# A two-layer hybrid mixer trunk: the first norm in two halves among the modulation loads, modulation by quarters, four c gates ahead of the scans' output, and later side steps

## The chip, the core and the metric

The kernel runs on one core of a Trainium2 chip. A core has five engines with queues of their own: TensorE (PE, matmuls; PEld is its weight load), VectorE (DVE), ScalarE (ACT), GpSimd (POOL) and SyncE (SP, which here only issues DMAs). The metric is the time of one execution on the device in microseconds, the median of several runs. The profile is of one such execution. TensorE's clock has two levels, 1.2 and 2.4 GHz; the profile gives the granted clock of a stretch as a share of the higher.

## The reference, cut to what matters

128 context tokens and 512 latent tokens of width 1024 go through two layers with the same weights; they are one block of 640 columns in the kernel. A layer is:

```python
sh1, sc1, g1, sh2, sc2, g2 = split(silu(c) @ w_mod + b_mod, 6)   # one row for context, one for latent
h = rmsnorm(x, norm1_g) * (1 + sc1) + sh1
proj = h @ w_in                                  # q k v, z, beta, a, hyena, fnet, gates a b c
y_a = delta_mixer(...)    # gated DeltaNet, chunks of 64, forward and backward scan
y_b = hyena_mixer(...)    # two long convolutions by FFT, filters from a small sine MLP
y_c = fourier_mixer(...)  # FNet
x = x + g1 * ((sig(ga) * (y_a @ w_pa) + sig(gb) * (y_b @ w_pb) + sig(gc) * (y_c @ w_pc)) @ w_o)
h = rmsnorm(x, norm2_g) * (1 + sc2) + sh2
x = x + g2 * (silu(h @ w_gate) * (h @ w_up)) @ w_down
```

The latent tokens first get a position embedding (`xs = x_sample + grid_pos_embed`). At the end stands one more rmsnorm; the final DeltaNet states of the context are an output too.

## The kernel before

Everything is transposed: the 1024 channels lie on 8 blocks of 128 partitions, the 640 tokens in the free dimension, in two chunks c=0 and c=1 of 320. A *main tile* is one weight tile of 128 output channels against all tokens. Operands are split in a high and a low part, and three products are added, so that a tile takes 8 x 3 x 2 = 48 matmuls of 128x320 into the PSUM tiles `pg`. Weights arrive in `wr` by SyncE's queue; `wh` (ScalarE) and `wl` (GpSimd, or an adding DMA that GpSimd issues) are their two parts. `_stream` lists the main tiles in the order in which they are run: `ba` and the q, k, v tiles (stage `qkv`), the FNet inputs and z (`fn`), twelve hyena tiles (`hy`), eight a gates (`ga`), two c gates, the merges of a, the rest of the c gates with the merges of c, b gates, merges of b, the o tiles, and the feed-forward half.

All other work is written as Python generators, *side steps*, in which each `yield` ends a step. `bg` puts one into a list; `pump`, called at several points of every main tile, takes those steps whose time `co.t` (plus the `hint` that was yielded) has come by the planner's own clock, up to a budget, and writes their instructions behind what is there. `on(...)` sets `co.t` to the time at which the planner expects the named tiles, and `self.cur.t += n` puts a step n of its microseconds later. All this happens while the program is written: on the chip each engine runs its own queue strictly in order, and semaphores tie the queues together. `finish` writes the remaining steps of a generator with no main tile between them.

The side steps of interest:
- `mods` computes the modulation `mod` (columns of w_mod against silu(c)): per group of four blocks two halves of small matmuls `ps<-A,ct`, a copy of the row by ScalarE into `U`, and two small matmuls (`ps<-small,U`, in `turn`) that turn it back into `mod`. With `first=True` 16 blocks are loaded ahead at the start; else 1 MB is loaded into one buffer for each half of a group.
- `embed` adds the positions to x and sums the squares (`sq_add`); `rstd` sums them over channels on TensorE (`ps<-small,T` 128x1), takes the rsqrt on VectorE with twelve tiny instructions (`nm`, `nr`, `rs`) and spreads it over the partitions with TensorE (`rb`, one tile `ps` per chunk); `norm` makes the gain `na` from `mod` and the normed tiles in high and low part.
- `filters` makes the hyena filters: a sine MLP (`sin_mlp`), then many steps of 2 to 6 matmuls.
- `delta_gates`, `delta_qk` (its `one(t)` normalises and transposes q and k for one of five blocks of tokens), `delta_unit` (the decay and key products of a chunk: GpSimd passes over 512 columns into `U`, matmuls with `stcr`, an exponential, products), `prep` (with `delta_inv`: inverses, on VectorE) and `scan` (33 numbered steps, each a few matmuls and VectorE operations, each needing the one before).
- `merge` multiplies a projected branch by its gate and adds it up; the last branch's sum is halved and split for the o tiles (`split`).

In `run`, the steps of `embed`, `mods` and `filters` before the first main tile are taken by `finish_one` in the planner's order, and the norm of x is begun only after that.

## Time and profile before

| | |
|---|---|
| median of three runs | 2749.7 us (2746.98 to 2753.47) |
| the profiled execution | 2748.93 us, its span 2747.2 us, granted clock 0.963 in the mean |
| TensorE busy | 2542.1 us, 93% of the span |
| VectorE / ScalarE / GpSimd busy | 1784.8 / 1101.5 / 1272.3 us, 65 / 40 / 46% |
| DMA | 353.57 MB, 129 GB/s in the mean |

TensorE is what the time is made of; the other engines matter where it waits for them. The idle time in front of a matmul, and what ended it, stands in brackets in TensorE's timeline. A busy time of TensorE has the clock in it: at the lower level the same matmul takes about twice as long.

The stages by time: start 0 to 54.4; layer 0: `qkv` to 239.9, `fn` to 325.0, `hy` to 467.1, `ga` to 557.1, then `dfin` (end of the scans, c gates), merges and gates, o tiles from 869.7 to 933.8, feed-forward half to 1398.5; layer 1: `qkv` to 1571.5, `fn` to 1669.5, `hy` to 1797.7, `ga` to 1916.5, o tiles from 2222.0 to 2285.8, feed-forward half to 2735.1.

### The profile page before, as it was taken

How to read it: one execution, taken by the hardware profiler on the slowest of the kernel's cores; microseconds unless marked ns; L12 is line 12 of the kernel's file. 1: busy time of each engine (PE TensorE's matmuls, PEld its weight loads, DVE VectorE, ACT ScalarE, POOL GpSimd, SP SyncE). 2: the span in 40 equal slices, each digit the busy share in tenths (PEclk: the TensorE clock that was granted, in tenths of full speed). 3: DMA queues.
4: the chain of work that ended last, by engine and by line, in shares of the span. 5: the costliest groups of instructions: out<-in, count | busy, mean ns of one | idle time of the engine just before them, and what ended most of it. 6: DMA issues, size and time to landing. Idle time of an engine off the chain costs nothing. (4 is left out here: it accounts for less than half of the span.)

```text
span 2747.2 us, 55957 instructions
## 1 busy us (share of the span) xinstructions
PE 2542.1 (93%) x22520; PEld 2411.4 (88%) x22520; DVE 1784.8 (65%) x3375; ACT 1101.5 (40%) x2383; POOL 1272.3 (46%) x1228
## 2 busy tenths in 40 slices
PE   5897999979999999999988989889999999999998
PEld 3786988979999999999977779778889998999997
DVE  5467977444645686667665789665456358777775
ACT  4454464422332343333335544534223333444442
POOL 2334325332335576666632352333333365776662
PEclk8998999989999999999989999989999999999999
DMA  7442663534554235422222437425255441222222
GB/s 295 171 164 63 162 146 90 155 134 146 204 191 169 62 128 173 162 78 85 85 97 90 144 79 184 115 65 159 95 200 193 163 167 47 85 85 77 85 76 79
DMA packets 125683, 353.57 MB, mean 129 GB/s; under 512 B 11994, under 2 KB 26330, under 8 KB 118944
## 3 DMA queue, kind: packets, MB, share of 16 engines
q1 hardware_dynamic: 107856, 312.76, 34.2%
q0 software_dynamic: 17568, 37.24, 7.1%
q8 instruction: 177, 2.90, 0.4%
q14 instruction: 82, 0.67, 0.1%
HBM read 288.60 MB, written 37.24 MB: 119 GB/s over the span
## 5 line engine op out<-in xcount | busy, mean ns | idle before, releaser
L2189 PE MATMUL pg<-A,wh 128*128 128x320 f32 (+1 forms) x6304 | 1456.0, 318 | 44.3 <-POOL A L2189 10.4
L2189 PEld LDWEIGHTS pg<-A,wh 128*128 128x128 f32 (+1 forms) x6304 | 1070.5, 192 | 87.0 <-POOL A L2189 18.0
L2189 PE MATMUL pg<-A,wl 128*128 128x320 f32 (+1 forms) x3152 | 990.5, 314 | 2.3 <-DMA wl<-wr 1.8
L2189 POOL TENSOR_TENSOR wl<-wr,wh 128x512 fp32r<-128x512 f32 (+2 forms) x374 | 524.3, 1415 | 513.8 <-ACT wh L2189 486.4
L2189 PEld LDWEIGHTS pg<-A,wl 128*128 128x128 f32 (+1 forms) x3152 | 603.5, 191 | 7.1 <-DMA wl<-wr 4.2
L2189 ACT CAST wh<-wr 128x512 fp32r<-128x512 f32 (+2 forms) x486 | 287.0, 609 | 278.8 <-PE pg L2189 231.4
L2189 PE MATMUL ps<-A,wh 128*128 128x320 f32 x1696 | 378.8, 310 | 0.0
L2189 PEld LDWEIGHTS ps<-A,wh 128*128 128x128 f32 x1696 | 283.9, 188 | 1.4 <-issue 1.0
L2189 PE MATMUL ps<-A,wl 128*128 128x320 f32 x848 | 263.5, 311 | 5.0 <-POOL wl L2189 4.8
L2189 POOL TENSOR_TENSOR wl<-U,wh 128x512 fp32r<-128x512 f32 x160 | 227.8, 1441 | 43.5 <-ACT wh L2189 43.5
L2189 POOL DMA_DIRECT2D wl<-wr x112 | 98.7, 912 | 277.7 <-ACT wl L2189 264.6
L2189 PE MATMUL ps<-A,A 32*32 32x32 f32 (+5 forms) x2984 | 205.3, 239 | 9.3 <-DVE A L2189 5.5
L2189 PEld LDWEIGHTS ps<-A,A 32*32 32x32 f32 (+2 forms) x2984 | 177.3, 142 | 20.2 <-DVE A L2189 6.0
L2189 DVE TENSOR_TENSOR T<-T,T 128x320 f32<-128x320 f32 (+1 forms) x139 | 133.6, 961 | 83.7 <-ACT T L2189 79.4
L2189 POOL TENSOR_TENSOR A<-A,A 128x640 fp32r<-128x640 f32 (+5 forms) x84 | 122.2, 1473 | 121.0 <-ACT A L2189 113.1
L2189 DVE TENSOR_TENSOR A<-A 128x120 f32<-128x120 f32 (+23 forms) x690 | 161.0, 297 | 14.0 <-DMA A<-hyS 10.8
L2189 PEld LDWEIGHTS ps<-A,wl 128*128 128x128 f32 x848 | 159.7, 188 | 7.4 <-POOL wl L2189 7.3
L2189 ACT CAST wh<-U 128x512 fp32r<-128x512 f32 x160 | 99.2, 621 | 165.4 <-PE ps L2189 60.0
L2189 PE MATMUL pg<-A,A 128*128 128x320 f32 x1056 | 161.0, 310 | 0.0
L2189 PEld LDWEIGHTS pg<-A,A 128*128 128x128 f32 x1056 | 156.3, 188 | 0.7 <-issue 0.2
L2189 DVE STREAM_TRANSPOSE A<-A 32x1024 f32<-32x1024 f32 x72 | 151.2, 2120 | 1.5
L2189 DVE TENSOR_TENSOR U<-ps,U 128x512 f32<-128x512 f32 x144 | 77.9, 542 | 103.3 <-PE ps L2189 66.8
(165 smaller groups left out, 3194.7 us busy)
## 6 DMA issues: line engine op xcount, KB each, us to landing
wr<-in_wbig_dram SPq DMA_DIRECT2D x272, 512.0 KB, 3.7
A<-in_wmod_dram SPq DMA_DIRECT2D x40, 1024.0 KB, 6.4
A<-hT SPq DMA_DIRECT2D x32, 1024.0 KB, 7.7
wl<-wr POOLq DMA_DIRECT2D x112, 256.0 KB, 4.5
kSp<-U SPq DMA_DIRECT2D x40, 256.0 KB, 2.0
U<-kSp SPq DMA_DIRECT2D x40, 256.0 KB, 8.7
A<-in_wmod_dram SPq DMA_DIRECT2D x16, 512.0 KB, 10.2
hyS<-T SPq DMA_DIRECT2D x24, 320.5 KB, 3.1
```

Of the source, the lines that this page charges most:

```text
L2189: return f(*a, **k)
```

## The change

- *Start.* `embed` is one step now, with all sums of squares; silu(c) is issued behind the table loads only; the groups of `mods` go in the order 0, 8, 4, 12, each turned at once. `norm` runs in two halves (`halves=True`): gain and tiles for channels 0 to 3 of both chunks between the groups, for 4 to 7 behind them. The order of the first steps is written out by hand in `run`. x is stored to DRAM (`xS`) behind the first tile's first chunk.
- *Modulation by quarters.* Outside the start a group is four steps with a load of 512 KB each, into two halves of a buffer in turn; the load of the next quarter is issued before the step of this one.
- *Four c gates* stand in front of the output of the scans; the first two c merges follow one another.
- *Merges by chunks.* The last branch's split is done for each chunk of 320; the factor 0.5 goes into the modulation gate `g`.
- *GpSimd.* The passes of `delta_unit` are three steps now instead of one; one subtraction of `filters` goes from VectorE to GpSimd.
- *Later steps.* `cur.t += 1.5` to `3.0` in `rstd` (not the first), `filters` of layer 1 (whose MLP is also cut into more steps), `delta_qk`, `delta_gates`, `delta_unit`, `hyena`.

The core of the diff:

```diff
 def _stream():
-    s += [gate("c", 0), gate("c", 1)]
+    s += [gate("c", m) for m in range(4)]
     s += [("pa", m) for m in range(0, 8, 2)]
-    s.append(("pc", 0))
-    for m in range(2, 8, 2):
+    s += [("pc", 0), ("pc", 2)]
+    for m in range(4, 8, 2):
         s += [gate("c", m), gate("c", m + 1), ("pc", m)]
...
 def mods(self, l, lo, hi, par=False, hint=0.5, first=False):
+        nq = 2 if first else 4
+        w1 = D // nq
...
+            js = js[::2] + js[1::2]
...
+            todo = [(j, h) for j in range(lo, hi, 4) for h in range(nq)]
+
+            def load():
+                j, h = todo.pop(0)
+                w = S[:, h % 2 * D:h % 2 * D + D]
+                nc.sync.dma_start(w.rearrange("p (g c) -> p g c", g=4),
+                                  self.I["wmod"][l, j:j + 4, :, h * w1:h * w1 + w1].rearrange("g p c -> p g c"))
...
-                    w = [S[:, g * 512:g * 512 + 512] for g in range(4)]
-                    nc.sync.dma_start(S[:, :2048].rearrange("p (g c) -> p g c", g=4),
-                                      self.I["wmod"][l, j:j + 4, :, h * 512:h * 512 + 512].rearrange("g p c -> p g c"))
+                    w = [S[:, h % 2 * D + g * w1:h % 2 * D + g * w1 + w1] for g in range(4)]
+                    if todo:
+                        load()
...
 def rstd(self, u, n, w):
         self.on(self.ssq[:, u:u + n * w])
+        if u:
+            self.cur.t += 3.0
         yield 0.0
...
 def norm(self, l, gcol, sh, scl, new, place, halves=False):
-        for c in range(2):
+        for k0, c in ((k0, c) for k0 in range(0, KD, n) for c in range(2)):
             yield from self.wait(c)
-            new(c)
-            for k in range(2):
+            if k0 == 0:
+                new(c)
+            if halves and c == 0:
+                gain(k0, n)
+            for k in range(k0, k0 + 2):
                 head(k, c)
...
 def filters(self, l):
+            if l:
+                self.cur.t += 3.0
             yield
+        for sl in (slice(0, TS), slice(TS, T)):
...
 def delta_unit(self, N, Pm, u, s, t):
             rhs.append(r)
+            self.cur.t += 1.5
+            yield
         E, mb = N[:, u], Pm[u]
...
+        yield
         ps = self.ps()
...
 def merge(self, br, m, th, first, last):
+                if last:
+                    hi, lo = [x[(m + i) // 4][:, (m + i) % 4][:, sl] for x in self.mgs]
+                    self.split(hi, lo, mt[:, sl], nc.vector if m == 6 else None)
                 self.pump()
-            if last:
-                hi, lo = self.mgs[0][(m + i) // 4][:, (m + i) % 4], self.mgs[1][(m + i) // 4][:, (m + i) % 4]
-                nc.vector.tensor_scalar(out=mt, in0=mt, scalar1=0.5, scalar2=None, op0=ALU.mult)
-                self.split(hi, lo, mt)
...
 def run(self):
+        self.rs, self.hn = [n, n], 0
+        co = self.co = self.bg(self.norm_mod(0, C_G1, 0, 8, True))
+        ff = self.ff
+        for x in (m, cd, ff, n, ff, m, m, n, n, ff, m, m, n, *[co] * 4, m, m):
+            self.step(x)
+        self.free(0, 0)
+        for x in (*[co] * 4, ff):
+            self.step(x)
+        while not m.done:
+            self.step(m)
```

How rows stand in the queues, at three places. First, VectorE at the start. `mod` is the modulation, `nm` and `nr` belong to the rsqrt, `T<-small,nr` is the tile that TensorE then spreads over the partitions, `na` is the gain, `U<-A,ps` the first normed tile. Before:

```order
L2189 TENSOR_TENSOR mod_114<-ps_371,par_90 128x2x4
L2189 TENSOR_TENSOR T_157<-T_157,T_374 128x640
L2189 TENSOR_TENSOR mod_114<-ps_395,par_90 128x2x4
L2189 TENSOR_SCALAR nm_404<-ps_398 128x5
L2189 TENSOR_SCALAR nr_405<-nm_404 128x5
L2189 TENSOR_TENSOR rs_407<-nr_405 128x5
...
L2189 TENSOR_TENSOR T_418<-small,nr_405 128x640
L2189 SCALAR_TENSOR_TENSOR na_446<-mod_114,par_90 128x8 x2
L2189 TENSOR_TENSOR U_453<-A_103,ps_420 128x320
L2189 TENSOR_TENSOR U_455<-A_103,ps_420 128x320
```
After, where the rows left out are the rsqrt's and two of the filters' sine:

```order
L2246 TENSOR_TENSOR mod_113<-ps_233,par_90 128x2x4
L2246 CAST stcr<-small 128x256
L2246 TENSOR_SCALAR nm_244<-ps_238 128x5
L2246 TENSOR_SCALAR nr_245<-nm_244 128x5
L2246 TENSOR_TENSOR rs_247<-nr_245 128x5
...
L2246 TENSOR_TENSOR T_258<-small,nr_245 128x640
L2246 TENSOR_SCALAR U_264<-U_263 128x512
...
L2246 TENSOR_SCALAR U_263<-U_263 128x512
L2246 TENSOR_TENSOR mod_113<-ps_312,par_90 128x2x4
L2246 SCALAR_TENSOR_TENSOR na_319<-mod_113,par_90 128x4 x2
L2246 TENSOR_TENSOR U_326<-A_106,ps_315 128x320
```
The rsqrt now stands behind the first `mod` group instead of the fourth, the gain is made of four columns behind the second group instead of eight behind the fourth, and the first tile follows it.

Second, GpSimd in `fn1`. The passes of a unit are `U<-dgh,small` (two) and `<-small,dsel`, `MEMSET A` clears the storage they end in, `DMA wl<-wr` adds a weight tile's low part. Before:

```order
L2189 DMA wl_17647<-wr_17177 128x512
L2189 DMA wl_17652<-wr_17177 128x512
L2189 MEMSET A_17781 128x1024
L2189 TENSOR_TENSOR U_17785<-dgh_16418,small 128x512
L2189 TENSOR_TENSOR U_17787<-dgh_16418,small 128x512
L2189 TENSOR_TENSOR U_17782<-small,dsel_16280 128x512
L2189 TENSOR_TENSOR U_17790<-dgh_16418,small 128x512
L2189 TENSOR_TENSOR U_17792<-dgh_16418,small 128x512
L2189 TENSOR_TENSOR U_17783<-small,dsel_16280 128x512
L2189 TENSOR_TENSOR A_17781<-A_17781,U_17782 128x512
L2189 TENSOR_TENSOR A_17781<-A_17781,U_17783 128x512
```
After:

```order
L2246 DMA wl_17664<-wr_17084 128x512
L2246 DMA wl_17669<-wr_17084 128x512
L2246 DMA wl_17837<-wr_17451 128x512
L2246 DMA wl_17842<-wr_17451 128x512
L2246 MEMSET A_17847 128x1024
L2246 TENSOR_TENSOR U_17851<-dgh_16531,small 128x512
L2246 TENSOR_TENSOR U_17853<-dgh_16531,small 128x512
L2246 TENSOR_TENSOR U_17870<-dgh_16531,small 128x512
L2246 TENSOR_TENSOR U_17872<-dgh_16531,small 128x512
L2246 TENSOR_TENSOR U_17848<-small,dsel_16408 128x512
L2246 TENSOR_TENSOR U_17849<-small,dsel_16408 128x512
L2246 TENSOR_TENSOR A_17847<-A_17847,U_17848 128x512
```
Another pair of weight loads stands ahead of the memset and the passes now; the passes of the two units alternate, and still follow one another.

Third, TensorE at the end of layer 1's `qkv`, where the filters' steps are `ps<-U,T` and `ps<-A,A` and main tiles are `pg`. Before:

```order
L2189 MATMUL ps_17038<-U_16836,T_16221 128x512
L2189 MATMUL ps_17038<-U_16837,T_16221 128x512
L2189 MATMUL pg_17054<-A_15731,wh_16816 128x320
L2189 MATMUL pg_17054<-A_15733,wh_16816 128x320
L2189 MATMUL pg_17054<-A_15731,wl_16817 128x320
L2189 MATMUL pg_17054<-A_15731,wh_16816 128x320
L2189 MATMUL pg_17054<-A_15733,wh_16816 128x320
L2189 MATMUL pg_17054<-A_15731,wl_16817 128x320
L2189 MATMUL ps_17061<-A_16687,A_16685 128x512
L2189 MATMUL ps_17061<-A_16688,A_16685 128x512
```
After, behind the last main tile of the stage:

```order
L2246 MATMUL ps_17181<-U_17035,T_16264 128x512
L2246 MATMUL ps_17181<-U_17036,T_16264 128x512
L2246 MATMUL ps_17188<-U_17035,T_16264 128x512
L2246 MATMUL ps_17188<-U_17036,T_16264 128x512
L2246 MATMUL ps_17195<-A_16890,A_16888 128x512
L2246 MATMUL ps_17195<-A_16891,A_16888 128x512
L2246 MATMUL ps_17195<-A_16890,A_16888 128x512
L2246 MATMUL ps_17202<-U_17035,T_16264 128x512
L2246 MATMUL ps_17202<-U_17036,T_16264 128x512
L2246 MATMUL ps_17218<-A_16890,A_16888 128x512
L2246 MATMUL ps_17218<-A_16891,A_16888 128x512
```
Six main matmuls stood between two filter steps; from here to the end of the stage there are none now.

## Rows read from the trace of the kernel before

**Rows 1.** The page: TensorE's busy time, share of the span, instructions.
```profile
PE 2542.1 (93%) x22520; PEld 2411.4 (88%) x22520; DVE 1784.8 (65%) x3375; ACT 1101.5 (40%) x2383; POOL 1272.3 (46%) x1228
```

**Rows 2.** Stretches: length, busy us of PE, PEld, DVE, ACT, POOL; PEclk, DMA.
```profile
0.00:54.40 54.40, 24.10 (x287) 16.70 (x287) 29.08 (x68) 15.54 (x31) 5.19 (x19) 0.84 0.84 323
...
54.40:239.90 185.50, 165.19 (x1080) 138.87 (x1081) 111.12 (x221) 99.85 (x238) 61.19 (x87) 0.93 0.44 148
...
1571.50:1669.50 98.00, 84.40 (x882) 80.24 (x880) 85.31 (x190) 44.96 (x88) 44.33 (x48) 0.93 0.46 113
...
1669.50:1832.40 162.90, 134.89 (x2123) 126.73 (x2121) 110.00 (x243) 78.73 (x204) 57.59 (x108) 0.91 0.50 119
```

**Rows 3.** TensorE's timeline, start: start, us, instruction, [idle before <- what ended it].
```profile
38.79 1.08 PE L2189 MATMUL ps<-A,ct 128*32 128x128 f32 x32
...
44.69 0.59 PE L2189 MATMUL ps<-small,U 128*128 128x8 f32 x2 [4.82 <-ACT U L2189]
...
50.96 2.47 PE L2189 MATMUL ps<-T,small 128*128 128x320 f32 x4 [3.21 <-DVE na L2189]
...
54.38 1.00 PE L2189 MATMUL pg<-A,wh 128*32 128x320 f32 x2 [0.94 <-ACT A L2189]
```

**Rows 4.** TensorE's timeline, three side steps in layer 0's `qkv`.
```profile
94.28 0.61 PE L2189 MATMUL ps<-small,T 32*128 32x32 f32 x5 [2.30 <-DVE T L2189]
...
211.96 0.63 PE L2189 MATMUL ps<-small,U 128*128 128x128 f32 x4 [3.25 <-DVE U L2189]
...
229.02 1.12 PE L2189 MATMUL ps<-small,A 128*128 128x128 f32 x4 [5.13 <-ACT A L2189]
```

**Rows 5.** TensorE's waits, whole span: us in total, times, longest.
```profile
PE ps L2189 <- POOL U L2189: 8.7, 11, 2.1
```

**Rows 6.** Timelines of VectorE, GpSimd and TensorE in `fn1`.
```profile
1594.78 6.78 DVE L2189 SCALAR_TENSOR_TENSOR dsr<-rs,dsr 128x16 f32<-128x16 f32 x1
...
1600.19 1.33 POOL L2189 TENSOR_TENSOR U<-small,dsel 128x512 f32<-128x512 f32 x1
...
1602.64 1.09 PE L2189 MATMUL ps<-small,U 128*128 128x128 f32 x4 [6.41 <-DVE U L2189]
```

**Rows 7.** Layer 1's scans: the stretch as in rows 2, then timelines.
```profile
1749.71:1832.40 82.69, 59.73 (x1514) 54.05 (x1513) 40.96 (x56) 32.70 (x86) 35.93 (x44) 0.81 0.27 68
...
1778.46 9.55 DVE L2189 SCALAR_TENSOR_TENSOR T<-T,par,T 128x641 f32<-128x641 f32 x2 [2.25 <-ACT T L2189]
...
1788.49 1.76 PE L2189 MATMUL ps<-A 64*64 64x64 f32 x28 [8.06 <-DVE A L2189]
...
1808.88 1.46 PE L2189 MATMUL ps<-A 64*64 64x64 f32 x18 [2.04 <-DVE A L2189]
...
1828.39 0.68 PE L2189 MATMUL ps<-A 64*64 64x64 f32 x16 [1.80 <-DVE A L2189]
```

**Rows 8.** Filters of layer 1: one wait of TensorE, and two stretches.
```profile
1483.18 0.48 PE L2189 MATMUL ps<-T,U 64*128 64x128 f32 x2 [3.87 <-ACT T L2189]
...
1525.25:1554.95 29.70, 29.70 (x151) 23.75 (x149) 19.63 (x28) 15.79 (x38) 10.96 (x18) 1.00 0.58 181
...
1554.95:1571.47 16.52, 14.74 (x53) 9.34 (x52) 11.95 (x16) 8.51 (x18) 5.67 (x6) 1.00 0.40 112
```

**Rows 9.** TensorE's timeline, first o tile of layer 0.
```profile
874.53 0.41 PE L2189 MATMUL pg<-A,wh 128*128 128x320 f32 x1 [1.49 <-ACT A L2189]
...
876.15 0.63 PE L2189 MATMUL pg<-A,wh 128*128 128x320 f32 x1 [1.20 <-POOL A L2189]
```

**Rows 10.** TensorE before `dfin0`; the page's DMA issues: KB each, us to landing.
```profile
557.08 1.93 PE L2189 MATMUL ps<-A,ct 128*32 128x128 f32 x32 [5.00 <-DMA A<-in_wmod_dram]
...
wr<-in_wbig_dram SPq DMA_DIRECT2D x272, 512.0 KB, 3.7
...
A<-in_wmod_dram SPq DMA_DIRECT2D x40, 1024.0 KB, 6.4
```

**Rows 11.** TensorE's timeline, start of layer 0's feed-forward half.
```profile
938.87 0.73 PE L2189 MATMUL ps<-small,T 128*80 128x1 f32 x8 [3.17 <-DVE T L2189]
```

115 lines of the change are left out of this document (67 added, 48 removed).

## The prediction

> **What bounds the kernel now.** The page comes first: TensorE is busy for 2542.1 us of a span of 2747.2 [rows 1], no other engine comes near that, and so the end moves with the 205 us in which TensorE stands still, and with the slow clock that goes with such places. Then the span is cut into the kernel's stages, to see which of them hold the idle time [rows 2]. At the start TensorE works 24.10 of 54.40 us, at a granted clock of 0.84; in layer 0's `qkv` stage 165.19 of 185.50; in `fn1` 84.40 of 98.00; from `hy1` to the first gate tile of layer 1 134.89 of 162.90, at 0.91. The feed-forward halves and the b gates are full and have little to give. In each loose stage TensorE's timeline shows the waits, and what ended each. They are nearly all waits of a *side step*, a few small matmuls that stand between the 48 of a main tile, on a helper engine that had been given too little time. Such a wait is a matter of order, and order is what the change alters.
>
> **The change, part by part.** Durations are those of one profiled execution (2748.93 us: a span of 2747.20 and 1.73 around it). The median of the runs is 2749.70, 0.8 above; the sum is put on the median.
>
> *Start: -6.* The last modulation matmuls end at 38.79 + 1.08 = 39.87, and nothing held them up, so their weights had landed. Then their row's copy comes 4.82 us late, rsqrt and gain take until 50.96, and the first main matmul goes at 54.38 [rows 3]: 14.5 us of chain. In the new order the rsqrt and the first four normed tiles stand ahead of the last two modulation groups; behind the last group come its copy (2 us at most, if nothing is queued ahead), its two small matmuls (0.59) and a gain, and the first main matmul reads tiles that are ready: 39.9 + 4 = 44, ten earlier. But the vector work that was behind the groups now stands between them, and VectorE and TensorE take turns there; I take -6, bounds 0 and -10. The 2.6 MB of x that are stored now leave later, behind the first tile, where no weight waits for them.
>
> *Layer 0, qkv and fn: -9.* Three side steps wait 2.30, 3.25 and 5.13 us [rows 4]: the gates' transposes and those of q and k. The new order puts 24 to 40 more matmuls (0.147 us each, a tile of 48 is 7.04) between each and its input, 3.5 to 6 us, so they should go: 10.7. The delta unit's matmuls wait for GpSimd 8.7 us in 11 places in both layers [rows 5], most of them in layer 0; with three more steps between passes and matmuls I count 7. What is late next is VectorE: in the same stretch of layer 1 it is busy for 85.31 of 98.00 us [rows 2], and its work on q and k gets no shorter, so a TensorE that is early meets it again. Half of 17.7, bounds +3 and -18.
>
> *Last merge tile (o0, o1): -6.* Its split was one pass over 640 columns after a scaling; it goes by chunks now, and the factor 0.5 moves into a small vector. 1.49 + 1.20 us go in layer 0 [rows 9], as much in layer 1, and some slow clock behind them. Bounds -4 and -8.
>
> *Layer 1, filters: +2.7.* Later filter steps end a wait of 3.87 us [rows 8]. But steps that are later have to stand somewhere: 29 of them now follow the last main tile of the stage, 13 before. Covered, 16 steps with 108 main matmuls took 29.70 us, or (29.70 - 108 x 0.147)/16 = 0.86 a step; without cover 13 took 16.52, or 1.27 [rows 8]. Sixteen more at a difference of 0.41 cost 6.6. Bounds -4 and +6.
>
> *GpSimd's passes (fn1): -5.* One vector instruction of 16 columns takes 6.78 us, and it ends as the last of six GpSimd passes ends, which ran without a pause; TensorE then waits 6.41 [rows 6]. In the new order the loads of the next weight tile stand ahead of these passes on GpSimd, so that they come about a tile (7 us) later, when this vector work is done. Bounds 0 and -7.
> The Trainium skill ("SBUF — State Buffer", section "Who interferes with whom") says that the port pair shared by the two engines is locked for one instruction, the other waiting until that has finished. The row speaks otherwise: 6.78 us is as long as the queue of passes, not as one of them. By the page's rule a block would end with one pass (1.33 in the row of GpSimd), spreading them would bring nothing here, and this term would be about -1.
>
> *Layer 1, scans (hy1, ga1): -13.* The steps #3 to #20 took from 1749.71 to 1832.40 [rows 7], 82.7 us, in which TensorE works 59.73 at a clock of 0.81; that is 4.6 us a step. 8.06 us of it is one wait, behind two vector instructions of 9.55 us together [rows 7]. Where no main tile stands among them, six steps took from 1808.88 to 1828.39 [rows 7], 3.25 each. In the new order the scans start 66 matmuls later (+9.5 us, less the 5 of `fn1`, so at 1754), and all but the first few have no cover: 17 x 3.25 = 55 us, and 6 for the last steps of the inverse, which now fall among them. The first gate tile would come at 1815, 17 us earlier: the main matmuls that covered the scans are done by then, so nothing is owed. Three scan steps now stand behind the last a gate, with pieces of the modulation: +4. Bounds -22 and +8.
>
> *Modulation by quarters: 0.* At the end of layer 0's scans two loads of 1 MB into one buffer cost 5.00 us [rows 10] and 4.57. Halves of that, two in flight, land in about 3.7 us in place of 6.4 [rows 10], but seven of them stand in a row now with no main tile between: (3.7 + 0.5) x 7/2 = 15 us with 4 of matmuls in it (a quarter takes half of the 1.08 of [rows 3]). So 10 us of waiting before and about 11 after. Bounds -5 and +6.
> The Trainium skill ("DMA: Bandwidth & Descriptors", section "Bandwidth") advises to batch transfers to 1 MiB and more. The rows agree as to the direction, 7.4 us for 1 MB in halves against 6.4; by that rule alone this term would be +1 to +2 where these loads are on the path.
>
> *The rest: 0.* The four c gates only lengthen the cover of the scans' output. A later `rstd` ends a wait of 3.17 us [rows 11] at each feed-forward half, but the second half's norm is then as much later, and its matmuls are due some 12 us on; bounds -6 and +5.
>
> Sum: -6 - 9 - 6 + 2.7 - 5 - 13 + 0 + 0 = -36.3, **2713 us**.
>
> **The rivals.** *A, the passes are no more apart than before.* On GpSimd's own queue they still stand one behind another; the new steps change their order and what is ahead of them. If the block comes back on another vector instruction, the 5 us of `fn1` and the 8.06 in the scans stay: 2713 + 13 = 2726. (The page's rule of one instruction gives the same time from the other side: blocks of 1.33 us that spreading can't shorten, and waits of 6.41 and 8.06 that have another cause and stay.) For it speaks the order; against it that VectorE's queue holds other work by then. 0.15.
> *B, slower, by the scans.* In `ga1` a scan's two GpSimd passes stand among a unit's four, and one of those waits for TensorE and ScalarE. If each unit holds a round of three steps up by its whole chain, a step goes from 3.25 to some 6.2 us: 17 x 6.2 = 105, the first gate at 1754 + 105 = 1859, 27 later than before, 40 more than I count: 2753. It decides from (1852 - 1754)/17 = 5.8 us a step, where the other gains (23) are eaten. The units stood among the six steps of 3.25 as well, which speaks against it. 0.11.
> *C, bound by VectorE.* What is won ahead of its chains (layer 0's 9, half of the start, the 5 and the 13) is given back there; -3 - 6 + 2.7 remain: 2743. For it speaks 85.31 of 98.00. 0.13.
> *D, order works in full.* Nothing is halved: 9 more in layer 0, 9 in the scans, 4 at the start: 2691. 0.13.
>
> **How the numbers follow.** The forecast, 2701 to 2725, has 0.48, and A, B, C and D the rest. The range leaves out B and the low half of D and reaches to C: 2692 to 2743. Within 0.2% (5.5 us, about what a measurement of this kernel can tell from no change) lie C's upper half and the beginning of B: 0.08. Slower: 0.08. Faster: 0.84.
>
> **What would show it.** First main matmul near 48; no wait of TensorE above 1 us that GpSimd's `U` ends; no vector instruction of 16 columns above 2 us in `fn1`; the filters' tail near 37 us; scans of layer 1 at 3.3 us a step, and their last stage's loads no longer than 15 us; no wait at the first o tile. I am wrong if scan steps take over 5.8 us, or if TensorE's idle time in `qkv0` (20.3 us, from [rows 2]) falls by less than 4.

## The result, and the profile after

The changed kernel takes 2778.58 us (2778.28 to 2782.72), the kernel before 2748.55 beside it: a ratio of 1.011 with a 95% interval of 1.0092 to 1.0127. It is 30 us slower, where 2713 was forecast and even the range ended at 2743. The direction is wrong, not only the size.

The profiled execution took 2778.82 us, its span is 2777.0. TensorE's line of the page, to be laid beside [rows 1]:

```profile
PE 2565.9 (92%) x22520; PEld 2421.1 (87%) x22520; DVE 1766.1 (64%) x3367; ACT 1107.5 (40%) x2398; POOL 1262.1 (45%) x1240
```

The same 22520 matmuls take 23.8 us more busy time at a lower clock (0.957 against 0.963), and idle time grows by 6. Stretches of the changed kernel, to be read as [rows 2] (length, then busy time of PE, PEld, DVE, ACT, POOL, then clock and DMA): the start, layer 0's `qkv` and `fn`, layer 1's `qkv` and `fn`, and from `hy1` to the first a gate of layer 1.

```profile
0.00:53.91 53.91, 25.53 (x287) 17.54 (x288) 32.01 (x75) 21.75 (x43) 10.44 (x20) 0.88 0.75 286
53.91:221.50 167.59, 155.34 (x1040) 131.72 (x1041) 93.41 (x175) 82.83 (x198) 54.42 (x90) 0.95 0.52 174
221.50:324.10 102.60, 81.85 (x843) 76.87 (x842) 79.81 (x174) 44.42 (x91) 46.24 (x51) 0.88 0.43 101
1405.42:1588.34 182.92, 157.51 (x821) 128.89 (x819) 111.95 (x190) 88.13 (x214) 62.07 (x102) 0.91 0.29 96
1588.30:1686.30 98.00, 84.19 (x882) 79.19 (x880) 78.61 (x185) 46.00 (x90) 43.80 (x47) 0.93 0.44 113
1686.30:1854.80 168.50, 138.27 (x2121) 129.53 (x2121) 102.54 (x247) 78.16 (x203) 58.25 (x108) 0.88 0.46 115
```

Cut by the first matmul of each stage, the span up to TensorE's last matmul stands as follows (us; some 7 follow in each kernel; `hy..pb` runs from the first hyena tile to the last merge of b). The last three columns are kernels of the next section. Each column is one profiled execution, and a stage whose lines do not differ can still vary by some 2 us (`o1` takes 60.4 in `b_merge` below and 62.7 in `b_merge_u1`), so differences of that size are not told from nothing.

| stretch | before | changed | difference | b_merge_u1 | u_later1 | u_later1f |
|---|---|---|---|---|---|---|
| start | 54.4 | 53.9 | -0.5 | 54.3 | 52.5 | 52.7 |
| qkv0 | 185.5 | 167.6 | -17.9 | 185.5 | 168.7 | 167.9 |
| fn0 | 85.1 | 102.5 | +17.4 | 85.1 | 103.1 | 102.6 |
| hy0..pb0 | 544.8 | 547.3 | +2.5 | 541.7 | 546.9 | 546.3 |
| o0 | 64.1 | 60.3 | -3.8 | 59.9 | 60.3 | 60.3 |
| ffn0 | 464.7 | 473.7 | +9.0 | 466.9 | 474.2 | 474.2 |
| qkv1 | 173.0 | 182.9 | +9.9 | 171.8 | 179.7 | 174.9 |
| fn1 | 98.0 | 97.9 | -0.1 | 101.9 | 104.0 | 105.0 |
| hy1..pb1 | 552.5 | 566.4 | +13.9 | 545.0 | 543.7 | 540.6 |
| o1 | 63.8 | 60.3 | -3.5 | 62.7 | 60.4 | 60.4 |
| ffn1 to last matmul | 454.6 | 457.3 | +2.7 | 455.9 | 457.3 | 457.9 |

Up to the o tiles of layer 0 the two kernels are level: 18 us won in `qkv0` are lost again in `fn0`. Nearly all that is lost, is lost in three places: layer 0's feed-forward half (+9.0), layer 1's `qkv` (+9.9) and layer 1's mixers (+13.9).

### The profile page after: what moved, and what is told of

It is laid out like the page before. It is cut to its first block, busy times and chain, and to the rows that moved or that the text cites. A ratio compares the mean times of both kernels' runs of the same rounds, so it can differ in the third digit from the quotient of the medians.

```text
span 2777.0 us, 56050 instructions
## 1 busy us (share of the span) xinstructions
PE 2565.9 (92%) x22520; PEld 2421.1 (87%) x22520; DVE 1766.1 (64%) x3367; ACT 1107.5 (40%) x2398; POOL 1262.1 (45%) x1240
## 5 line engine op out<-in xcount | busy, mean ns | idle before, releaser
L2246 POOL TENSOR_TENSOR wl<-wr,wh 128x512 fp32r<-128x512 f32 (+2 forms) x374 | 518.4, 1400 | 527.0 <-ACT wh L2246 504.2
L2246 PE MATMUL ps<-A,A 32*32 32x32 f32 (+5 forms) x2984 | 212.3, 245 | 18.7 <-DVE A L2246 7.8
L2246 PEld LDWEIGHTS ps<-A,A 32*32 32x32 f32 (+2 forms) x2984 | 183.4, 147 | 32.4 <-DVE A L2246 8.1
L2246 DVE TENSOR_TENSOR T<-T,T 128x320 f32<-128x320 f32 (+1 forms) x139 | 131.3, 945 | 85.1 <-ACT T L2246 80.4
L2246 DVE TENSOR_TENSOR A<-A 128x120 f32<-128x120 f32 (+23 forms) x690 | 174.6, 320 | 5.9 <-POOL A L2246 2.1
L2246 POOL TENSOR_TENSOR A<-A,A 128x320 fp32r<-128x320 f32 (+5 forms) x92 | 118.2, 1296 | 125.0 <-ACT A L2246 103.8
L2246 DVE SCALAR_TENSOR_TENSOR T<-T,par,T 128x641 f32<-128x641 f32 x84 | 105.0, 1249 | 83.8 <-POOL T L2246 42.3
```

What stands on the lines that cost most here:

```text
L2246: return f(*a, **k)
```

## Experiments

Names that begin with `u_` are the changed kernel with one part undone, names with `b_` (and `a_start`) the kernel before with one part added; `b_merge_u1`, `best2` and `u_later1f` combine two or three edits. All compute the whole of the reference. Ratios are against the kernel before, timed beside each; the changed kernel itself stands at 1.011.

**What each part costs when it is undone.** First the quarters: two halves of 1 MB a group again, loaded into one buffer.

```diff
-        nq = 2 if first else 4
+        nq = 2
...
-                    if todo:
-                        load()
+                    w = [S[:, g * w1:g * w1 + w1] for g in range(4)]
```


> The changed kernel with one part undone: outside the start a modulation group is again two steps with 1 MB loads into one buffer. Theory 1 (each part costs in its own place): the feed-forward half of layer 0, where 16 steps were cut into 32, gets 5 us shorter (473.7 to about 469), the ends of the scans some 3 us; in all -8 us against the changed kernel (2778.6), about 2770. Theory 2 (helper chains set the time, and order only moves the waits about): within 3 us of 2778.6, the feed-forward half unchanged.


Measured: 2798.7, ratio 1.0175 [1.0155, 1.0195], 20 us slower than the changed kernel and no gain. `ffn0` does fall, from 473.7 to 468.6. But the edit also moves side steps elsewhere: in layer 0 scan step #3 stands 72 matmuls later in TensorE's order (place 2234, not 2162; the trace's own count of matmul records is higher than these places by the same 509 in layer 0 and 2390 in layer 1 in every kernel), and `hy0..pb0` grows by 27.1. One part can't be taken out of this kernel without moving others; from here on each run is read by stretch.

Then the filters' delay in layer 1 and the delays in `rstd` (two places each, of which one is shown), and the order at the start (the last modulation group ahead of the norm's second-chunk tiles and of a filter step):

```diff
-            if l:
-                self.cur.t += 3.0
...
-        if u:
-            self.cur.t += 3.0
...
-        for x in (*[co] * 4, ff):
-            self.step(x)
         while not m.done:
             self.step(m)
+        for x in (*[co] * 4, ff):
+            self.step(x)
```


> The changed kernel without the delay of 3.0 for the filter steps of layer 1 (the cut into more steps and the subtraction on GpSimd stay). Theory 1: the uncovered tail of layer 1's qkv stage (29 steps, 40 us) falls back to about 13 steps and the stage from 182.9 us to 173, so about 2768. Theory 2: the wait comes back in another place (ScalarE's evictions behind the sine), stage 180 or more, time within 3 us of 2778.6.


Measured: 2773.9, 1.0077 [1.0057, 1.0098]. `qkv1` falls from 182.9 to 177.5: 5.4 of its +9.9 go with the filters' delay. The whole falls by 4.7 by the medians and 9 by the ratios.


> The changed kernel without the delays of 3.0 in rstd. Theory 1: the second half's norm is in time again; the two feed-forward halves lose 4 and 3 us, the stage qkv of layer 1 about 1: 2771. Theory 2: the waits of 3.2 us at the start of each half come back and cancel that: 2777 to 2780.


Measured: 2780.6, 1.0114 [1.009, 1.0137], no difference that could be told. `ffn0` falls by 1.4, so this delay is not what `ffn0` lost.


> The changed kernel with the last modulation group's steps ahead of the four norm steps of the second chunk and of the filters' sine, so that ScalarE copies that group's row without them in its queue. Theory 1: the wait of 8.33 us before the first main matmul shrinks to 2, first main matmul at about 47.5 in place of 53.9, and 3 to 6 us of it reach the end: 2773 to 2776. Theory 2: the second chunk's norm is late instead, first main matmul earlier but the c=1 matmuls wait, 2778.


Measured: 2786.5, 1.0124 [1.0106, 1.0143]. The first main matmul comes 9.3 us sooner, and a wait of 7.14 stands nine microseconds behind it. TensorE's timeline of this kernel, as [rows 3]:

```profile
43.83 0.39 PE L2246 MATMUL ps<-small,U 128*128 128x8 f32 x2 [0.47 <-ACT U L2246]
...
44.56 0.48 PE L2246 MATMUL pg<-A,wh 128*32 128x320 f32 x2
...
53.64 0.47 PE L2246 MATMUL pg<-A,wh 128*32 128x320 f32 x1 [7.14 <-ACT A L2246]
```
ScalarE has the row's copy early now (until 43.77) and the norm's other tiles late. Of the 9.4 us from there to the cast at 53.13 it stands idle for 5.0 (1.83, 0.27, 2.19 and 0.75), waiting for VectorE, so this is not ScalarE's work alone: the order of VectorE's has a part in it. 4.4 us of the rest go in `qkv0`, and more in `hy0`, where the first a gate comes 152.9 us behind the first hyena tile instead of 142.3.

**What each part brings alone.** The merge by chunks, the quarters, the start, the four c gates, and the delays in `delta_qk`, `delta_gates` and `hyena`, each added to the kernel before with the lines of the diff ahead of the prediction. (The bare `yield` that this diff shows under `delta_unit` belongs to `delta_gates`; the cut of the units is the `yield` inside the loop over two passes.)


> The kernel before with one part of the change alone: the last merge split by chunks, 0.5 in the modulation gate. My prediction's term: -6 (o0 and o1 3 to 3.8 us shorter each, nothing given back), 2743. Rival, from the trace of the changed kernel: the norm of the feed-forward half's second chunk runs on VectorE at its own pace and is read at once, so that what TensorE gains in o0 and o1 it waits for in the half's first tiles; o stages 3.7 us shorter, halves 2 to 3 us longer, in all -1 to -3.


Measured: 2743.2, 0.9978 [0.9966, 0.9989]. `o0` falls from 64.1 to 59.6, `o1` from 63.8 to 60.4, and `ffn0` takes 2 back. This term of the sum holds.


> The kernel before with one part alone: modulation by quarters outside the start. If each step that cuts a main tile open has its own price (0.3 us for each of 16 more steps), the feed-forward half of layer 0 is 5 us longer and dfin0's two waits of 5 us become shorter: in all 0 to +5. If instead the quarters matter by where the scans then fall (the changed kernel without quarters was 20 us slower than with them), hy0 and ga0 change by more than 5 us either way.


Measured: 2768.0, 1.0061 [1.0047, 1.0076]. `ffn0` grows from 464.7 to 472.3 and `qkv0` by 8, where TensorE waits 10.78 at 132.32 for a filter step. So the quarters cost 7.6 in `ffn0` alone, where `u_quarters` gave back 5.1; what each is made of comes below.


> Only the start of the change (embed in one piece, norm in two halves, groups in the order 0, 8, 4, 12, x stored later), the rest as before. My prediction's term: first main matmul near 48, all of it kept, -6: 2743. From the trace of the changed kernel: first main matmul at 53 to 54, since ScalarE copies the last group's row only behind the second chunk's tiles and the filters' sine; then 0 from the start, and whatever the other order does to hy0 and ga0: between -5 and +15.


Measured: 2771.6, 1.0077 [1.0063, 1.0091]. The first main matmul comes 1.6 earlier and `qkv0` grows by 13. In this kernel the parts of the filters' MLP that were moved with the start are in it too, in layer 1 as well, and there `qkv1` grows by 6.9 without any delay. Timelines of TensorE and VectorE:

```profile
110.44 1.51 PE L2221 MATMUL ps<-U,T 128*128 128x512 f32 x2 [9.83 <-DVE U L2221]
...
101.86 0.68 DVE L2221 TENSOR_TENSOR U<-U,A 1x512 f32<-1x512 f32 x1 [8.06 <-DMA A<-in_fb_dram]
```
TensorE waits for a vector operation that stands in VectorE's queue behind one that waits 8.06 us for a load.


> The kernel before with one part alone: four c gates ahead of the scans' output, the first two c merges in a row. My prediction's term: 0 (a better cover for the output of the scans, -1). From the trace of the changed kernel, where the stages from the first a merge to the last b merge are 2.3 us longer for the same work: +2 a layer, since the hyena steps reach the b gates, with waits of 1.8 us there: 2753.


Measured: 2754.7, 1.0012 [1.0002, 1.0022], some 3 us slower.


> The kernel before with one part alone: the delays in delta_qk (2.0), delta_gates (2.5 and a step more) and hyena (1.5). My prediction: the side steps' waits in layer 0's qkv stage go, -5 here, 2744. Rival: the other parts of the change, each alone, sum to far more than the +30 measured; then this part must bring much, -20 or more, or the parts undo one another, and it is near 0 alone (2746 to 2756) with the waits moved on into fn0.


Measured: 2763.9, 1.0045 [1.003, 1.0059]. `qkv0`, for which these delays were meant, stays at 185.1; `qkv1` grows by 5.1. In `fn1` the wait of 6.41 and the long vector instruction of [rows 6] are gone, and the stage takes 98.1, as before.

**The passes of a unit.** The cut with the delay of 1.5 that belongs to it (`b_units`), and the cut alone, without the middle line (`b_unityield`):

```diff
             rhs.append(r)
+            self.cur.t += 1.5
+            yield
```


> The kernel before with one part alone: the GpSimd passes of delta_unit in three steps. My prediction's term: the vector instruction of 6.78 us in fn1 is gone, fn1 5 us shorter. Rival (passes that stand later are waited for by TensorE): a wait of 6 to 9 us that GpSimd's U ends appears in fn1, as in the changed kernel (8.96), and fn0; layer 1's scans start later; in all 0 to +8.


Measured: 2784.9, 1.012 [1.0098, 1.0142].


> As the run with delta_unit's passes in three steps (2784.9), but without the delay of 1.5 between them: only the cut into steps is left. If the delay puts layer 0's scans too late (first scan matmuls 25 us later, first a gate 26 us later), this is near 2750 again. If the cut alone does it, since each yield lets other steps in, first a gate of layer 0 stays at 160 us or more behind the stage's start (before: 142), and the time above 2765.


Measured: 2759.8, 1.0028 [1.0016, 1.004]. The two differ in layer 0: with the delay scan step #3 stands at place 2234 and the first a gate comes 168.7 us after `hy0` begins, without it at 2156 and 145.0. In layer 1 both bring `hy1..pb1` down, to 542.1 and 544.1, and both raise `fn1` to 103 to 105. So the delay is what costs in layer 0; what is won in layer 1's scans comes with the cut alone, and the delay adds 2 us at most.

So it was tried in layer 1 only, with the merge by chunks:

```diff
+            if self.dl:
+                self.cur.t += 1.5
+                yield
```


> Towards a version that beats both: the kernel before with the merge by chunks, and delta_unit's passes in three delayed steps in layer 1 only. In the run with both layers, layer 1 took 10 us less from hy1 to the first a gate and 7 more in fn1; layer 0 is left as before here. Against 2743.2 with the merge alone: -3, so 2740, if the two layers are independent; 2743 or more if what fn1 loses is as much.


Measured: 2736.6, ratio 0.9945 [0.9931, 0.9958]. This kernel beats both: by the ratio 15 us ahead of the kernel before. It is two pieces of the change, and the table above shows where they stand: `o0` -4.2, `hy1..pb1` -7.5, and `fn1` +3.9. The early start added to it, with the last modulation group first, takes the gain away again:


> The kernel before with merge by chunks, the units' delay in layer 1 only, and the change's start with the last modulation group ahead of the second chunk's norm steps and of the sine. Against 2736.6 without the start: first main matmul at 44.6 in place of 54.4; if what follows keeps it, -7 to -9 (2728); if a filter step then waits for its base's load, as when the start stood alone (9.83 us in qkv), 2735 to 2742.


Measured: 2749.4, 0.9987 [0.9978, 0.9996]. The start falls from 54.3 to 46.2, `qkv0` grows from 185.5 to 198.5 (layer 0's part of the MLP moves with the start here too).

**What puts layer 1's scans late.** In layer 1 the place of scan step #3 in TensorE's order went with the loss, and neither the units' delay alone (11612) nor the later steps alone (11702, as before) put it late in layer 1; the changed kernel has 11768. So each of the two was taken out of the changed kernel: the first two lines of this diff (in `delta_unit`) in `u_units`, the rest (in `delta_qk`, `delta_gates` and `hyena`) in `u_later`.

```diff
             rhs.append(r)
-            self.cur.t += 1.5
-            yield
...
-            self.cur.t += 2.0
...
-        self.on(ba[:32])
-        self.cur.t += 2.5
-        yield
...
-            self.cur.t += 1.5
```


> The changed kernel with delta_unit's passes in one step again. The first scan matmul stands at index 2204 in layer 0 (2162 in the changed kernel) and 11702 in layer 1 (11768). If this place sets the first a gate: layer 0 some 12 us later than in the changed kernel, layer 1 about 6 earlier, at +163 from the stage's start, and fn1 without its wait of 8.96: about 2778. If units are the loss by themselves, as alone (+36): 2750 to 2760.


Measured: 2770.8, 1.0076 [1.0058, 1.0094]; place 11702, `hy1..pb1` 553.5 instead of 566.4.


> The changed kernel without the delays in delta_qk, delta_gates and hyena. The first scan matmul stands at 2108 in layer 0 and 11612 in layer 1, earlier than in any other. If this place sets the first a gate: layer 1 at +152 to +155 from the stage's start in place of +168.5, layer 0 no later than +142, fn0 or fn1 some 5 us longer by the units' waits: about 2762. If the delays hide more waits than they cost (layer 0's qkv stage is 18 us shorter in the changed kernel): 2780 or more.


Measured: 2760.5, 1.0035 [1.0023, 1.0047]; place 11612, `hy1..pb1` 542.8. But `qkv0` grows from 167.6 to 196.4 (and `fn0` falls from 102.5 to 93.3): beside the new start the later steps are worth 20 us up to the end of layer 0's `fn`, of which 13 go again in `hy0..pb0`; in layer 1 they cost 24 in `hy1..pb1` and save 6 in `fn1`.

Last, the same with layer 0 left alone, and then the filters' delay taken out as well:

```diff
-            self.cur.t += 2.0
+            if not self.dl:
+                self.cur.t += 2.0
...
-        self.on(ba[:32])
-        self.cur.t += 2.5
-        yield
+        if not l:
+            self.on(ba[:32])
+            self.cur.t += 2.5
+            yield
...
-            self.cur.t += 1.5
+            if not l:
+                self.cur.t += 1.5
```


> The changed kernel, but the steps of the gates, of q and k and of the hyena branch come late in layer 0 only; in layer 1 they stand as before the change. Layer 0 is word for word that of the changed kernel. Theory (in layer 1 the delay in the units and the later steps together push scan step #3 behind 66 more matmuls, to place 11768 of TensorE's order; with one of the two alone it stands at 11612 to 11702): here it stands at 11612, so that the first a gate comes 151 to 154 us after the start of hy1 instead of 168.5, the stretch hy1 to pb1 falls from 566.4 to 543 to 546, qkv1 falls by some 3 and fn1 grows by 4 to 6 as its waits come back: 2778.6 - 22 - 3 + 5 = 2758, between 2753 and 2763. Rival (VectorE's conv work and the inverses, in lockstep with the main tiles of hy1, set the pace, and the place of the scans in the order follows only on paper): the first a gate stays at +163 to +170 and the time within 5 us of 2778.


Measured: 2759.7, 1.0027 [1.0017, 1.0036]: 19 us, or by the ratios 23 us, under the changed kernel. `hy1..pb1` is 543.7, `fn1` 104.0, `qkv1` 179.7, the first a gate comes 152.1 us behind `hy1`'s first tile. They lie where the theory put them (`fn1`, at +6.1, a tenth beyond), and the times that the rival gave are excluded. Its lockstep of VectorE and the main tiles is not: the edit takes that away together with the place, as the part on layer 1's scans shows.


> As the one before, and layer 1's filter steps also come without the 3 us of delay. Theory (the filters' delay costs by itself, through 29 steps without cover at the end of qkv1): qkv1 falls by another 3 to 5.5 us, the rest stays: 2758 - 4 = 2754, between 2749 and 2759. Rival (both edits mend the same queue of late steps, so that the second brings nothing more): within 1.5 us of the one before.


Measured: 2754.8, 1.0013 [1.0001, 1.0024]. `qkv1` falls by another 4.8: the two edits add up.

The gap between the last hyena tile and the first a gate, 34.6 us in the kernel before, 55.9 in the changed kernel and 13.7 in `u_later1`, shows what the place does. The greater part of it as stretches, in this order:

```profile
1797.70:1832.40 34.70, 23.94 (x806) 21.38 (x805) 19.68 (x38) 12.03 (x35) 19.35 (x19) 0.80 0.18 43
```
```profile
1802.57:1854.80 52.23, 37.58 (x1225) 34.01 (x1225) 23.53 (x45) 17.88 (x48) 27.80 (x28) 0.71 0.11 30
```
```profile
1829.30:1841.50 12.20, 8.42 (x358) 7.56 (x354) 9.38 (x17) 5.95 (x16) 7.75 (x8) 1.00 0.49 116
```
Ten, thirteen and four of the scan steps #3 to #19 stand in these stretches with no main tile among them. The later the scans begin in the order, the fewer main tiles are left to cover them.

## Why the prediction was wrong, point by point

**Start: -6, measured -0.5.** The step that failed is "its copy (2 us at most, if nothing is queued ahead)". Things are queued ahead. TensorE's timeline, then ScalarE's, of the changed kernel:

```profile
53.46 0.60 PE L2246 MATMUL ps<-small,U 128*128 128x8 f32 x2 [8.33 <-ACT U L2246]
...
48.34 0.65 ACT L2246 ACTIVATE U<-U,mod,na 128x320 f32<-128x320 f32 x1
...
49.38 0.45 ACT L2246 ACTIVATE U<-ps,fbb 128x128 f32<-128x128 f32 x1
52.16 0.31 ACT L2246 ACTIVATE U<-U 128x128 f32<-128x128 f32 x1 [2.32 <-DVE U L2246]
...
53.14 0.27 ACT L2246 COPY U<-ps 128x128 f32<-128x128 f32 x1
```
The last copy takes 0.27 us, and stands behind the second chunk's norm tiles and a sine step of the filters, in which ScalarE itself waits 2.32 for VectorE. TensorE's last modulation matmuls are done near 45. I had read VectorE's and TensorE's order there, and not ScalarE's. `u_start` mends exactly that and gains nothing in the end, so neither of these two orders brings the -6; part of what `u_start` gives back goes with layer 0's scans, which stand 12 places later in it.

**Layer 0: -9, measured -0.5 over `qkv0` and `fn0`.** The three waits of [rows 4] are gone from their places, as forecast, and TensorE's idle time in `qkv0` fell from 20.3 to 12.3 us, more than the 4 that I had asked for. The waits came back behind it. TensorE's timeline, waits over 2.5 us to the end of `fn0`:

```profile
104.64 0.56 PE L2246 MATMUL ps<-small,U 128*128 128x8 f32 x2 [3.64 <-DVE T L2246]
...
130.36 2.93 PE L2246 MATMUL ps<-A,A 128*128 128x512 f32 x6 [5.67 <-DVE U L2246]
...
227.54 1.11 PE L2246 MATMUL ps<-small,A 128*128 128x128 f32 x4 [4.51 <-ACT A L2246]
...
238.76 1.11 PE L2246 MATMUL ps<-small,A 128*128 128x128 f32 x4 [7.55 <-ACT A L2246]
...
285.38 0.80 PE L2246 MATMUL ps<-U,stcr 128*128 128x512 f32 x1 [6.25 <-POOL U L2246]
```
The transposes of q and k, 5.13 at 229.02 before, now wait 4.51 and 7.55, for copies of ScalarE, in whose queue the step just ahead had waited 9.53 and 4.56 us for VectorE. This looks like rival C, in this one place: a TensorE that is early meets the helpers' chain. C was given 0.13 and a gain of 9 halved beside it; here nothing is left. That the chain sets the end of `fn0` is argued, not shown, and VectorE is no limit by its busy time (79.81 of 102.60). What the runs show is a sum that the prediction did not make: the new start alone adds 15 us to the two stages (`a_start`), the later steps alone bring nothing (`b_later`, +0.5), and beside the new start they are worth 20 (`u_later`).

**Merge: -6, measured -3.8 and -3.5**, the waits of [rows 9] are gone, and `b_merge` shows it alone. In `b_merge` 2 us come back in layer 0's feed-forward half, which the sum had not, and none in layer 1's.

**Modulation by quarters: 0, measured +3.5 to +4, in a stage that I had not looked at.** At the end of layer 0's scans the loads did as forecast. Waits there, and the page's line on these loads, as [rows 10]:

```profile
557.45 1.08 PE L2246 MATMUL ps<-A,ct 128*32 128x128 f32 x16 [3.17 <-DMA A<-in_wmod_dram]
...
563.37 0.87 PE L2246 MATMUL ps<-A,ct 128*32 128x128 f32 x12 [3.30 <-DMA A<-in_wmod_dram]
565.33 1.08 PE L2246 MATMUL ps<-A,ct 128*32 128x128 f32 x16 [0.88 <-DMA A<-in_wmod_dram]
...
A<-in_wmod_dram SPq DMA_DIRECT2D x96, 512.0 KB, 4.5
```
7.35 us, against 9.57 before and some 11 forecast. The price is paid in `ffn0`, where 16 halves become 32 quarters among the main tiles of a full TensorE. One of each, with the matmul behind it (before, then changed):

```profile
987.14 1.08 PE L2189 MATMUL ps<-A,ct 128*32 128x128 f32 x32
988.15 0.56 PE L2189 MATMUL ps<-A,wh 128*128 128x320 f32 x2
```
```profile
990.29 0.64 PE L2246 MATMUL ps<-A,ct 128*32 128x128 f32 x16
990.86 0.57 PE L2246 MATMUL pg<-A,wh 128*128 128x320 f32 x2
```
Half the matmuls take 0.57 from start to start, not half of 1.01, and the break ahead of them, 0.09 in both kernels, is paid again: 0.13 + 0.09 = 0.22 for each of 16 more breaks, 3.5 in all. `b_quarters` has 7.6 us more in `ffn0`, of which 3.4 is time lost to the low clock (below), so 4.2, or 0.26 each; against `u_quarters` the changed kernel has 5.1, of which 1.7 is clock, so 0.21 each. The sum costed the loads and not the cuts.

The other part of `ffn0`'s +9.0 is TensorE's clock. Stretches of 8 us, 20 behind the start of `ffn0`, changed kernel and then before:

```profile
951.73:959.73 8.00, 7.15 (x24) 5.94 (x25) 7.83 (x11) 3.31 (x7) 6.73 (x7) 0.57 0.00 0
```
```profile
953.78:961.78 8.00, 7.66 (x53) 7.40 (x52) 7.96 (x7) 3.23 (x7) 8.00 (x6) 1.00 0.01 2
```
At a clock of 0.57 the 8 us do the work of 4.6. Over the whole stage the changed kernel loses 5.1 us to the lower level, the kernel before 1.7. The later `rstd` is not the cause. It did end the wait of [rows 11], but `u_rstd`, which has that wait back (3.18), loses the same 5.1, only sooner; 4 us behind the start of its `ffn0`:

```profile
932.90:940.90 8.00, 6.93 (x32) 6.93 (x33) 3.67 (x13) 3.00 (x5) 3.21 (x3) 0.57 0.24 68
```
`b_merge` and `b_quarters`, with the old `rstd` and a wait of 3.17, fall there as well; the kernel before, with the same wait, does not. So 3.4 of the +9.0 are a clock that fell in one profiled execution and not in the other, for a reason that stays open; 3.5 to 4 are the breaks, and the rest, 1.5 to 2, has no row of its own. The delay in `rstd` is worth nothing that can be told: `ffn0` is 1.4 shorter without it.

**Filters: +2.7, measured +9.9 in `qkv1`.** The direction held, and 5.4 of it goes with the delay (`u_filters`; 4.8 in `u_later1f`), 3.2 with the later steps of layer 1 (`u_later1`). The tail of 29 uncovered steps took 43.22 us, 1.49 each, where 1.27 had been taken from [rows 8] and 37 forecast: it contains a new wait of 3.73, and its clock is 0.88, where the tail before had 1.00. Without either delay (`u_later1f`) the tail is as short as before. The other thing that the sum lacked is a wait of main matmuls, ahead of the tail. TensorE's timeline, ScalarE's, and the tail as a stretch:

```profile
1497.90 0.90 PE L2246 MATMUL pg<-A,wh 128*128 128x320 f32 x2 [7.52 <-ACT T L2246]
...
1556.24 0.50 PE L2246 MATMUL ps<-U,T 128*128 128x512 f32 x1 [3.73 <-ACT U L2246]
...
1494.68 0.63 ACT L2246 ACTIVATE U<-U 128x512 f32<-128x512 f32 x1 [3.60 <-DVE U L2246]
...
1496.66 0.27 ACT L2246 COPY T<-pg 128x128 f32<-128x128 f32 x1
...
1545.12:1588.34 43.22, 35.73 (x111) 22.58 (x110) 28.28 (x38) 16.59 (x32) 11.89 (x11) 0.88 0.40 131
```
ScalarE, which also empties the tiles `pg`, stands 3.60 us in a sine step that waits for VectorE; the eviction behind it comes late, and 48-matmul tiles wait 7.52. This wait does not need the delay: `a_start`, whose MLP is cut without it, has main tiles waiting 4.18 and 2.72 for such evictions (1.56 before), a tail as short as before, and `qkv1` at +6.9; `best2`, with layer 1's MLP uncut, has none over 1.2 there, but `b_later`, with the MLP uncut as well, has 5.29 and 4.01. So the shares above, got by undoing, are not parts of one fixed sum. The step that failed: the move of a filter step was costed on TensorE and not on the queue in which its sine stands ahead of evictions.

**GpSimd's passes: -5 in `fn1`, measured -0.1.** The block of [rows 6] is gone: no vector instruction of 16 columns in `fn1` is longer than 0.2 us, and the wait of 6.41 is 2.25. A wait of 8.96 has taken its place. Timelines of TensorE, GpSimd and VectorE:

```profile
1657.24 0.80 PE L2246 MATMUL ps<-U,stcr 128*128 128x512 f32 x1 [8.96 <-POOL U L2246]
...
1655.05 1.16 POOL L2246 MEMSET A<- 128x1024 f32 x2 [9.88 <-DVE A L2246]
1656.14 2.05 POOL L2246 TENSOR_TENSOR U<-dgh,small 128x512 fp32r<-128x512 f32 x2
...
1659.27 1.29 POOL L2246 TENSOR_TENSOR A<-A,A 128x512 f32<-128x512 f32 x1
...
1629.95 0.43 DVE L2246 TENSOR_TENSOR U<-ps,A 128x256 f32<-128x256 f32 x1 [12.60 <-POOL A L2246]
...
1633.87 14.61 DVE L2246 STREAM_TRANSPOSE A<-A 32x1024 f32<-32x1024 f32 x7
...
1656.25 0.98 DVE L2246 TENSOR_TENSOR A<-A 128x31 f32<-128x31 f32 x1 [0.86 <-POOL A L2246]
...
1659.30 1.33 DVE L2246 TENSOR_TENSOR A<-A 128x60 f32<-128x60 f32 x1
```
VectorE stands idle for 12.60 us until GpSimd has ended the first units, then has 25 us of transposes, sums and copies in a row; GpSimd waits 9.88 for one of them, to clear a tile, and only then come the passes for which TensorE stands. The order that I read showed that the passes moved behind a weight load; it did not show for whom GpSimd itself would wait. TensorE's waits for GpSimd's `U`, 8.7 us in 11 places before [rows 5], are more now:

```profile
PE ps L2246 <- POOL U L2246: 19.3, 9, 9.0
```
The step that failed is the price: the 6.41 of one wait was taken for time on the path. `b_later` and `u_units` have the passes in one step, no such block (no vector instruction of 16 columns over 0.2 us) and no wait above 3.60 in `fn1`, and still take 98.1 and 98.2; so it was not the passes alone that moved the block, and its going is worth nothing in this stage. The passes cut, in the kernel before, cost 5 to 7 us there (`b_unityield`, `b_units`), with waits of 6.70 and 6.19 for GpSimd.

Short vector instructions are held up still, as rival A had it: the four from 1656.25 to 1660.63 (31 and 60 columns) take 0.98 to 1.33 each, where later ones with no such pass beside them take some 0.3. No wait of TensorE above 0.6 us follows them in `fn1`. The prediction weighed a rule of the Trainium skill here ("SBUF — State Buffer", "Who interferes with whom": the shared port is locked for one instruction), by which this term would have been about -1. These rows agree with the rule: each of the four ends 0.05 to 0.08 us behind one GpSimd pass (1657.23 behind 1657.18, 1660.63 behind 1660.56), held for one pass and not for the queue. The row of 6.78 in [rows 6], one instruction over six passes, does not fit it; what decides between the two, no run here settles. That the time came out near the -1 is not owed to the rule.

**Layer 1, scans: -13, measured +13.9 over `hy1..pb1`.** Four steps of the working can be laid beside the trace. *The place:* 66 matmuls later, right. *The start:* "+9.5 us" counts those 66 at 0.147; measured, scan step #3 starts 102.3 us behind `hy1`'s first tile instead of 80.2, that is 22 later. Main tiles of 7.04 us of matmuls take about 10 each there. Timelines of SyncE, ScalarE, GpSimd, and VectorE with its convolutions of main tiles:

```profile
1725.71 10.16 SPq L2246 DMA_DIRECT2D hyS<-T  x2
1736.03 0.83 SPq L2246 DMA_DIRECT2D wr<-in_wbig_dram  x2
...
1740.74 0.64 ACT L2246 ACTIVATE wl<-wr 128x512 fp32r<-128x512 f32 x1 [6.23 <-DMA wr<-in_wbig_dram]
...
1741.67 0.87 POOL L2246 DMA_DIRECT2D wl<-wr  x1 [8.02 <-ACT wl L2246]
...
1733.64 1.81 DVE L2246 SCALAR_TENSOR_TENSOR T<-T,par,T 128x641 f32<-128x641 f32 x2 [2.63 <-POOL T L2246]
...
1743.76 1.81 DVE L2246 SCALAR_TENSOR_TENSOR T<-T,par,T 128x641 f32<-128x641 f32 x2 [4.29 <-POOL T L2246]
```
This is a ring of queues. Two stores of hyena tiles stand in SyncE's queue, the second waits for the convolution at 1733.64, and the loads of the next weights stand behind it; ScalarE waits 6.23 us for these weights, GpSimd 8.02 for ScalarE, and behind that load GpSimd clears the edges for which the next convolution waits 4.29. So VectorE starts a convolution every 10 us and is idle for 2.6 to 4.3 of them, while the inverse's steps stand in its queue behind the next one. This order, two stores and then two loads, comes four times running in `hy1` of the changed kernel and of the four others whose scan step #3 stands at 11768, where ScalarE waits 18.5 to 20.8 us for weights up to the first a gate; in the kernel before and in all the others it comes once, with 3.7 to 7.6. The prediction had no row of this queue. *The pace:* 3.25 a step from six steps of [rows 7]; 17 steps (#3 to #19) took 66.2 us from 1788.6, or 3.9, since the first of them, still in the inverse, wait 5.59 once:

```profile
1811.10 6.85 PE L2246 MATMUL ps<-A,A 32*32 32x32 f32 x254 [5.59 <-DVE A L2246]
...
1841.09 1.15 PE L2246 MATMUL ps<-A 64*64 64x64 f32 x32 [2.61 <-DVE A L2246]
```
So rival B's slow pace (over 5.8) did not come. (The 82.7 us before hold 17 steps as well, up to the start of #20, so they were 4.9 a step and not 4.6; the forecast does not hang on that.) Laid from `hy1`'s first tile, the forecast had the first gate at about 89.5 + 61 = 150.5; it came at 102.3 + 66.2 = 168.5, and 12.8 of the 18 is the start. *What follows:* behind the first a gate 8.3 us more than before (397.9 against 389.6), where +4 was taken for the three scan steps and the quarters behind the a gates.

Behind all this is a wrong sign. "The main matmuls that covered the scans are done by then, so nothing is owed" is true only if those matmuls ran at full pace before, and they didn't. A later scan loses its cover and wins nothing. The kernels with the scans *earlier* are the quicker ones: place 11612 gives the first a gate at +150 to +153 in six kernels, 11654 +153.9 in one, 11702 +161 to +165 in seven, 11768 +165 to +170 in the changed kernel and the four that undo another part of it. `u_later1` and `u_units` move this place in the changed kernel, and the time follows. From 11612 to 11702 the place stands without the ring; from there to 11768 the ring comes with it, and no run here parts the two: 66 matmuls are 9.7 us of the 22 that step #3 starts later.

**The rest: 0.** The four c gates cost some 3 us alone, the delay in `rstd` nothing that can be told.

**The sum.** -0.5 - 0.5 - 7.3 + 9.0 + 9.9 - 0.1 + 13.9 + 2.7 and +2.5 in layer 0's mixers are 29.6; the spans differ by 29.8. The five terms forecast as gains, -39, came to +5.5; the others, +2.7, to +24.1. What stays open: why `ffn0` lost its clock, how much of `hy1..pb1` is the place and how much the ring, and that the parts are not additive. Alone, the six that were tried add some 80 us to the kernel before (by their ratios), together 30, since each moves the planner's places for the others' steps. For layer 1's scans the pair of edits that does it was found; why the units' delay puts layer 0's scans at place 2234, and why they do not stand there when the quarters are beside it, was not settled.

## What to carry to other kernels

A step that is moved later has to be costed in every queue that it stands in, above all the one that empties another's buffers (here ScalarE's evictions behind a sine, and SyncE's weight loads behind stores), and the question for each wait taken away is which helper is late next, not how long the wait was. A long serial chain, such as these scans, is best begun where most full-size work is still to come: with its place in the order `hy1..pb1` went from 543.7 (`u_later1`) to 566.4 us here, the ring included. Changes to a planner's times should be tried one at a time and by layer: two pieces of this change, one of them in one layer only, gain 15 us, and the whole costs 30.

## What the runs showed of the hardware

TensorE's clock fell in the longer of the stretches without main tiles above: it was granted 0.80 over 34.7 us, 0.71 over 52.2, and 1.00 over 12.2. Near the start of `ffn0` it was granted 0.57 over 8 us in the changed kernel and `u_rstd`, 0.57 to 0.58 in `b_merge` and `b_quarters`, and 1.00 in the kernel before; one long wait or several short ones ahead of it made no difference that could be told. Breaking into a stream of full matmuls cost 0.22 us a time here: 0.09 ahead of the small matmuls, and 0.13 because the same ones in two pieces take 2 x 0.57 instead of 1.01. Vector instructions of 31 and 60 columns were held for one GpSimd pass each (0.98 to 1.33 us, in `fn1` of the changed kernel), one of 16 columns for six passes (6.78, in the kernel before).
